# A 3x3 convolution with 2x2 max pooling: a new program order, 21 column maxima as one reduction, and sums placed on other engines

## The chip, the core and the metric

The kernel runs on one core of one Trainium2 chip. The core has five engines, each with a queue of its own that it works through in order: TensorE (PE in the profile; its weight loads are shown as PEld), VectorE (DVE), ScalarE (ACT), GpSimd (POOL) and SyncE (SP). An instruction waits for semaphores that other engines raise, and all that stands behind it in its queue waits with it. The metric is device time in microseconds. The time of a kernel is the median of several executions, and one further execution is profiled. The span of the profile runs from the first to the last instruction of the core.

## What is computed

The input x is 16 images of 64 channels and 64x64 points, the weight is 128x64x3x3. The kernel convolves with a border of one zero and takes the maximum of each 2x2 block:

```python
x_pad = np.pad(x, ((0, 0), (0, 0), (1, 1), (1, 1)))
...
conv[b, co] += weight[co, ci, kh, kw] * x_pad[b, ci, kh:kh+h, kw:kw+w]
...
output[b, c, i, j] = np.max(conv[b, c, 2*i:2*i+2, 2*j:2*j+2])
```

The output is 16x128x32x32 in float32, and on the chip x and the weights are rounded to bfloat16.

## The kernel before

**Tiles.** Two images lie on the 128 partitions together, 64 channels each, so there are 8 pairs of images (`xb_0` to `xb_7`). Each pair is cut into 4 strips of 16 rows, which gives 32 strips. Strip s belongs to pair s // 4; strips 2 and 3 trade places. For a strip and a half h (one image of the pair), 8 pooled rows of 64 columns fill one PSUM bank of 512 float32 numbers. There are 8 banks, and the program hands them out from a list of free ones (`take`, `free`).

**Products.** A strip needs the even and the odd convolution rows, and only their maximum counts. Both share a common part, which is added after the maximum of rows, because max(u+c, v+c) = max(u, v)+c. In a strip of type K (strips 0, 2, 4, 10, 16, 23) there are five products for each half: PA1 and PA2 into one bank, PB1 and PB2 into another, and PR, the common part, on the sum of rows `ks`. In a strip of type W (the other 26) there are four: P2 on a difference of rows (`we`, step E), P0 and P3 on a larger difference (`wd`, step D), P1 on a sum of rows (`ws`, step S). A product is three matmuls (kernel columns 1, 0 and 2; 512, 504 and 504 output columns, line 182). The matmul of half 0 and that of half 1 use different rows of the array and are issued in turn, one of each; `product` (line 236) holds a product back until the other half has one too. The first three strips (F, H, G) and the last (Z, Q) use products over half a strip.

**Steps of a strip after TensorE.** SE (line 356, ACT) copies the bank of P2 to a second bank, so that P0 adds to the one and P3 to the other. EV (lines 340 and 342, ACT) copies the first bank to SBUF as `ev` and frees it. MX (line 376, DVE) takes the maximum of the second bank and `ev` in place, and P1 (or PR) then adds to it. OD (line 382, ACT) copies the odd columns, 256 numbers per partition, to `od`. CM (line 396, DVE) takes the maximum of the even columns in PSUM and `od` into the output tile `o`, and frees the bank. ST (line 416) stores a strip over SP's queue. The output tiles are a ring of 12 (line 61): the 13th strip's first CM waits until the first strip's store has landed.

**Engines of the sums.** E, S, D and the halves Ea, Eb, Da, Db of strip 1 run on DVE or, where `ON_GPSIMD` names them, on POOL. A sum on POOL is made to wait for the last sum that stands before it in the order on DVE (`behind`, lines 74 to 84).

**Weights and loads.** The weights arrive in one transfer, are cast (g0, g1, g2), combined (D2, D0, GS, GM, GP), transposed on TensorE (TD2 to TMP, line 149) and copied back from PSUM (VD2 to VMP, lines 164 to 168) by ACT or DVE. The loads of x are issued by POOL (line 105): seven for pair 0 (La to C), two or three for each other pair (LX.p.part). So a load also waits its turn in POOL's queue.

**Order.** All of this is one list of 749 steps, `ORDER`, written out by hand, and each engine's queue is the part of the list that concerns it. At the start 8 matmuls on constants (line 524) run before any data is there.

Of the kernel before, what the change touches and what calls it, by code (L numbers as in the profile page):

```python
# [11 lines left out]
def kernel(  # L12
# [451 lines left out]
    for m in PRODUCTS:  # L464
# [13 lines left out]
        OD.3.1 CM.3.1 E.7 P2.7.0 P2.7.1 SE.7.0 P1.5.1 P1.5.0 S.9 S.6 P1.6.0 LX.5.0 P1.6.1 S.7 SE.7.1 P3.7.0
        P0.7.0 E.11 E.9 P2.9.0 PA1.10.0 OD.5.0 CM.5.0 OD.6.1 CM.6.1 E.13 OD.5.1 CM.5.1 OD.6.0 CM.6.0 KS.10 D.13
        S.14 E.8 P0.7.1 EV.7.1 P3.7.1 MX.7.1 EV.7.0 MX.7.0 P2.9.1 SE.9.0 PA1.10.1 PA2.10.1 SE.9.1 P0.9.1 P3.9.1  # L480
        PA2.10.0 EV.10.0 D.11 S.8 S.11 P0.9.0 EV.9.0 P3.9.0 MX.9.0 PB1.10.0 P1.7.1 PB1.10.1 PB2.10.0 PB2.10.1
        P2.8.1 EV.9.1 MX.9.1 OD.7.1 CM.7.1 P1.7.0 P1.9.0 P1.9.1 P2.13.0 MX.10.0 PR.10.0 P2.8.0 EV.10.1 MX.10.1
        PR.10.1 PA1.16.0 PA2.16.0 OD.7.0 CM.7.0 ST.0 ST.2 ST.6 D.8 SE.8.1 OD.9.0 CM.9.0 P0.8.1 LX.5.1 S.13
        LX.6.0 OD.9.1 CM.9.1 OD.10.0 CM.10.0 OD.10.1 CM.10.1 ST.10 PA1.16.1 PA2.16.1 D.17 D.12 D.14 S.15 P3.8.1
        SE.8.0 P0.8.0 EV.8.1 MX.8.1 SE.13.0 EV.16.1 EV.16.0 EV.8.0 P3.8.0 P0.13.0 P2.11.1 PB1.16.1 P2.11.0
        PB2.16.1 E.17 EV.13.0 P1.8.1 SE.11.1 P0.11.1 P3.11.1 P3.13.0 MX.8.0 P1.8.0 SE.11.0 P0.11.0 P3.11.0 E.20
        KS.16 MX.16.1 PR.16.1 MX.13.0 OD.8.1 CM.8.1 OD.8.0 CM.8.0 EV.11.1 MX.11.1 EV.11.0 MX.11.0 P2.13.1
        OD.16.1 CM.16.1 P1.13.0 OD.13.0 CM.13.0 PB1.16.0 PB2.16.0 E.14 P2.14.1 P1.11.0 P2.14.0 P1.11.1 SE.13.1
        P0.13.1 MX.16.0 SE.14.1 P3.13.1 P0.14.1 OD.11.1 CM.11.1 OD.11.0 CM.11.0 E.15 E.18 LX.6.1 E.12 P3.14.1
        PR.16.0 P2.12.1 P2.12.0 EV.13.1 SE.14.0 P0.14.0 D.18 KS.23 MX.13.1 P1.13.1 P3.14.0 EV.14.1 MX.14.1  # L490
        P1.14.1 S.19 S.20 SE.12.0 P0.12.0 EV.14.0 MX.14.0 SE.12.1 P3.12.0 P0.12.1 OD.16.0 CM.16.0 EV.12.0
        MX.12.0 OD.14.1 CM.14.1 EV.12.1 OD.13.1 CM.13.1 ST.5 ST.13 P3.12.1 P1.14.0 OD.14.0 CM.14.0 ST.14 ST.7
        ST.16 ST.3 P2.18.0 S.12 P1.12.0 P2.15.0 P2.17.1 PA1.23.1 SE.18.0 PA2.23.1 MX.12.1 P1.12.1 OD.12.0
        CM.12.0 E.19 S.17 LX.7.0 LX.7.1 D.15 D.20 D.24 SE.17.1 EV.23.1 P0.18.0 P0.17.1 EV.18.0 SE.15.0 OD.12.1
        CM.12.1 P3.18.0 MX.18.0 P3.17.1 P2.17.0 PB1.23.1 P2.18.1 PB2.23.1 EV.17.1 MX.17.1 P1.17.1 P0.15.0
        SE.17.0 P3.15.0 EV.15.0 MX.15.0 SE.18.1 P0.18.1 P0.17.0 P3.17.0 S.18 P1.18.0 P1.15.0 P3.18.1 MX.23.1
        P2.15.1 EV.17.0 MX.17.0 P1.17.0 PR.23.1 OD.17.1 CM.17.1 OD.18.0 CM.18.0 EV.18.1 MX.18.1 PA1.23.0
        PA2.23.0 P1.18.1 OD.15.0 CM.15.0 OD.17.0 CM.17.0 ST.11 ST.12 ST.9 S.22 D.25 E.22 D.19 S.24 SE.15.1
        OD.23.1 OD.18.1 CM.18.1 P2.20.0 P0.15.1 P2.19.1 PB1.23.0 PB2.23.0 P3.15.1 E.25 EV.23.0 CM.23.1 SE.20.0
        P0.20.0 P3.20.0 MX.23.0 PR.23.0 P2.19.0 P2.20.1 SE.19.1 P0.19.1 P3.19.1 EV.15.1 MX.15.1 P1.15.1 EV.20.0  # L500
        MX.20.0 P1.20.0 SE.20.1 P0.20.1 P2.22.0 OD.23.0 CM.23.0 ST.23 ST.18 ST.8 EV.19.1 MX.19.1 OD.15.1 CM.15.1
        SE.19.0 P0.19.0 P3.20.1 EV.20.1 MX.20.1 SE.22.0 OD.20.0 P1.19.1 D.21 E.21 P3.19.0 P2.22.1 D.22 P0.22.0
        P3.22.0 P1.20.1 E.24 CM.20.0 S.26 EV.19.0 MX.19.0 P2.21.1 P1.19.0 OD.19.1 CM.19.1 SE.22.1 P0.22.1
        P3.22.1 OD.20.1 CM.20.1 ST.20 S.29 EV.22.0 MX.22.0 SE.21.1 P2.24.0 P0.21.1 P3.21.1 EV.22.1 MX.22.1
        P2.21.0 OD.19.0 CM.19.0 P1.22.0 P1.22.1 SE.24.0 P0.24.0 EV.21.1 MX.21.1 OD.22.0 CM.22.0 P2.24.1 P2.25.1
        P3.24.0 SE.21.0 OD.22.1 CM.22.1 S.25 S.21 S.28 P0.21.0 P3.21.0 P2.25.0 P1.21.1 E.26 E.28 EV.24.0 MX.24.0
# [59 lines left out]
```

## Time and profile before

| what | before |
|---|---|
| median of 3 executions | 101.95 us (101.53 to 102.34) |
| profiled execution | 101.44 us, of it the span 99.7 us |
| busy, of the span | PE 94.1, PEld 60.8, DVE 86.2, ACT 83.2, POOL 72.8 us |
| mean granted TensorE clock | 0.99 |
| DMA | 17.23 MB, mean 173 GB/s |

The profiled execution lies 0.51 us below the median. What lies outside the span (1.7 us) is taken as fixed. An engine that is busy all the time need not be the one that sets the end; for that one looks at who waits for whom. The busy time of a group is given with the mean duration of one instruction; where instructions of an engine follow one another directly, each starts some 0.05 to 0.1 us before the one ahead of it has ended, so what an instruction occupies is the distance of two starts.

### The profile page before, as it was taken

The numbers are of one execution on the slowest core, as the hardware profiler recorded it, in microseconds if no ns is written. First come the engines' busy times: TensorE is split into PE (matmuls) and PEld (weight loads), VectorE is DVE, ScalarE is ACT, GpSimd is POOL, SyncE is SP. The second block draws the span as 40 slices with busy tenths as digits, with TensorE's granted clock in tenths as the row PEclk, the third lists the DMA queues.
The fourth block names the chain that finished last, engine by engine and source line by source line (L and its number), as shares of the span: only waits on it lengthen the run. The fifth ranks groups of instructions, "written<-read, shape, count | busy, mean of one in ns | idle before, by whom it ended". The sixth has DMA issues, their size and how long they took to land.

```text
span 99.7 us, 2526 instructions
## 1 busy us (share of the span) xinstructions
PE 94.1 (94%) x913; PEld 60.8 (61%) x913; DVE 86.2 (86%) x192; ACT 83.2 (83%) x192; POOL 72.8 (73%) x74
## 2 busy tenths in 40 slices
PE   6999999999999999999999999999999999998830
...
DVE  3568899999999999999999999889896899888660
...
GB/s 57 167 170 157 184 203 208 205 221 207 227 230 230 263 276 197 183 229 77 144 3 285 147 205 227 357 187 180 105 105 7 68 268 193 0 217 105 138 202 81
DMA packets 12316, 17.23 MB, mean 173 GB/s; under 512 B 912, under 2 KB 10256, under 8 KB 12304
## 3 DMA queue, kind: packets, MB, share of 16 engines
...
q8 instruction: 7, 0.11, 0.5%
...
## 4 chain that ended last, share of the span: by engine, by line
PE 83%; ACT 9%; DVE 3%; issue 1%; DVEq 0%; ACTq 0%
PE acc L182 78%; ACT ev L342 4%; PE acc L524 4%; ACT acc L356 3%; PE acc L149 2%; ACT od L382 2%; DVE acc L376 1%; DVE acc L372 1%; DVE o L396 0%; DVE o L410 0%; ACT od L402 0%; DVEq L561 0%; DVEq L376 0%; ACTq L356 0%
## 5 line engine op out<-in xcount | busy, mean ns | idle before, releaser
L182 PEld LDWEIGHTS <-wt 64*128 64x128 bf16 x882 | 57.8, 94 | 31.5 <-issue 3.9
L182 PE MATMUL acc<-wd,wt 64*128 64x512 bf16 (+3 forms) x330 | 60.0, 365 | 0.0
L376 DVE TENSOR_TENSOR acc<-acc,ev 128x512 f32<-128x512 f32 x62 | 41.4, 694 | 3.8 <-ACT ev L342 2.0
L182 PE MATMUL acc<-ws,wt 64*128 64x512 bf16 (+3 forms) x162 | 37.4, 369 | 1.0 <-DVE acc L372 0.7
L182 PE MATMUL acc<-we,wt 64*128 64x512 bf16 (+3 forms) x162 | 36.6, 369 | 0.0
L342 ACT ACTIVATE ev<-acc 128x512 f32<-128x512 f32 x52 | 31.0, 617 | 0.6 <-PE acc L182 0.3
L356 ACT COPY acc<-acc 128x512 f32<-128x512 f32 x48 | 28.3, 595 | 3.1 <-DVE o L396 1.6
L396 DVE TENSOR_TENSOR o<-acc,od 128x256 f32<-128x256 f32 x62 | 24.5, 417 | 1.9 <-ACT od L382 1.3
L89 POOL TENSOR_TENSOR ws<-xb 128x512 bf16<-128x512 bf16 x18 | 20.6, 1155 | 6.5 <-PE acc L182 4.5
L89 POOL TENSOR_TENSOR we<-xb 128x512 bf16<-128x512 bf16 x17 | 19.5, 1154 | 7.6 <-DVE wd L88 3.9
L382 ACT COPY od<-acc 128x256 f32<-128x256 f32 x62 | 22.7, 389 | 2.2 <-PE acc L182 1.6
L89 POOL TENSOR_TENSOR wd<-xb 128x1024 bf16<-128x1024 bf16 (+1 forms) x10 | 20.3, 2030 | 5.2 <-DVE we L88 5.2
L182 PE MATMUL acc<-xb,wt 64*128 64x252 bf16 (+7 forms) x192 | 23.9, 319 | 0.0
L105 POOL DMA_DIRECT2D xb<-in_x_dram x22 | 12.2, 567 | 0.8 <-POOLq L547 0.8
L88 DVE TENSOR_TENSOR wd<-xb 128x1024 bf16<-128x1024 bf16 (+1 forms) x17 | 10.8, 667 | 0.0
L340 ACT COPY ev<-acc 128x512 f32<-128x512 f32 x12 | 6.7, 595 | 3.1 <-PE acc L182 3.1
L182 PE MATMUL acc<-ks,wt 64*128 64x504 bf16 (+1 forms) x36 | 7.3, 377 | 0.0
L524 PE MATMUL acc<-const-bfloat16-1.0 128*128 128x512 bf16 x8 | 3.6, 625 | 0.8 <-PEq L547 0.8
L88 DVE TENSOR_TENSOR we<-xb 128x512 bf16<-128x512 bf16 (+1 forms) x10 | 3.7, 391 | 0.0
L88 DVE TENSOR_TENSOR ws<-xb 128x512 bf16<-128x512 bf16 x8 | 3.3, 418 | 0.0
L88 DVE TENSOR_TENSOR ks<-xb 128x512 bf16<-128x512 bf16 x6 | 2.6, 438 | 0.7 <-DMA xb<-in_x_dram 0.7
L524 PEld LDWEIGHTS <-const-bfloat16-1.0 128*128 128x128 bf16 x8 | 1.0, 136 | 2.4 <-issue 2.4
...
## 6 DMA issues: line engine op xcount, KB each, us to landing
...
```

Source lines behind the costliest of these rows:

```text
L88: return on_vector(nc.vector.tensor_tensor(**args))
L89: return on_gpsimd(nc.gpsimd.tensor_tensor(**args))
L105: nc.gpsimd.dma_start(out=xb[p][:, 1 + lo : 1 + hi, :], in_=rows_of(p, lo, hi))
L149: nc.tensor.transpose(tp[:, k * CO : (k + 1) * CO], wq[:, j : j + 2, :].rearrange("a b c -> a (b c)"), ident,)
L182: nc.tensor.matmul(acc[t][:, i0:i1, o0:o1], wt[lo : lo + CI, m0 + kw - h, :], rows(lo, i0, i1, c0, c1), start=start and kw == 1, stop=True ...
L340: nc.scalar.copy(out=ev[s, h], in_=acc[t])
L342: nc.scalar.mul(ev[s, h], acc[t], -1.0)
L356: nc.scalar.copy(out=acc[tb[s, h]], in_=acc[ta[s, h]])
L376: nc.vector.tensor_tensor(out=t, in0=t, in1=ev[s, h], op=MAX)
L382: nc.scalar.copy(out=od[s, h], in_=acc[tb[s, h]][:, :, 1::2])
L396: nc.vector.tensor_tensor(out=ot[s][:, h], in0=acc[t][:, :, 0::2], in1=od[s, h], op=MAX)
L524: nc.tensor.matmul(acc[n].rearrange("p a b -> p (a b)"), ones[:, 0:128], ones, start=True, stop=True, skip_group_check=True)
```

## The change

- `REDUCED` was empty and now names 21 (strip, half) pairs. For these OD is left out, and CM is one `tensor_reduce` with maximum over pairs of neighbouring columns: it reads all 512 numbers of the bank and writes 256 (lines 388 to 395, present before but not reached).
- `ON_GPSIMD`: E.9, E.20, E.25, E.26, E.28, S.1, S.7, S.19, S.20 and Db go from DVE to POOL; E.5, S.5, S.18, S.25, S.27, S.28 and Da go from POOL to DVE. GS goes from POOL to DVE.
- ACT takes over the cast g1 and the copies VG1, VG2 and VMP from DVE.
- The list has the same 749 steps in another order.
- `last_start` and the branches for a last strip of type K are new, but the last strip stays W and no step Y stands in the list, so they change no instruction.

Some facts of the two lists. TensorE gets the same 882 matmuls; the last 126, from P2.27 on, stand in the same order except that P1.28.1 and P2.29.1 trade places. Between MX.13.0 and MX.26.0, both included, in the middle of the list:

| steps from MX.13.0 to MX.26.0 | before | after |
|---|---|---|
| matmuls from the end of P3.13.0 to the end of P3.26.0 | 354 | 354 |
| DVE: MX / CM as maximum / CM as reduction | 30 / 30 / 0 | 30 / 14 / 16 |
| DVE: sums D / other sums | 5 / 9 | 5 / 7 |
| ACT: EV / SE / OD | 28 / 25 / 30 | 27 / 25 / 13 |

The stores of the first strips stand later in the list: before, ST.4 and ST.1 stand just after CM.4.0, and after, the first ones (ST.3 ST.2 ST.0 ST.1) stand after CM.10.0.

The diff, with the list cut to its first and last lines and to those that the prediction speaks of:

```diff
@@ -38,13 +38,13 @@
 
     TYPES = "KWKWKWWWWWKWWWWWKWWWWWWKWWWWWWWW"
     ON_GPSIMD = """
-        Da E.3 S.3 E.5 S.5 E.6 E.7 S.9 S.6 E.13 D.11 S.8 S.11 S.13 E.17 E.14 E.15 E.18 E.12 S.12 E.19 S.17 S.18
-        S.22 D.25 E.22 D.21 E.21 D.22 S.26 S.25 S.21 S.28 D.26 D.28 E.27 E.29 D.27 E.30 S.27 D.30 S.30 E.31 D.31
-        S.31
+        Db S.1 E.3 S.3 E.7 E.6 S.6 E.9 S.7 E.13 S.9 S.8 S.11 D.11 S.13 S.20 E.14 E.12 E.17 S.17 E.18 E.20 E.15
+        S.12 S.19 E.19 S.22 E.22 E.29 D.25 D.22 E.21 D.21 E.28 E.27 S.21 E.25 E.26 D.26 S.26 D.28 D.27 E.30 D.30
+        E.31 S.30 D.31 S.31
     """.split()
-    TURNED_BY_SCALAR = ("D2", "G0", "D0")
-    CAST_BY_SCALAR = ("g0", "g2")
-    REDUCED = ()
+    TURNED_BY_SCALAR = ("D2", "G1", "G0", "D0", "G2", "MP")
+    CAST_BY_SCALAR = ("g0", "g1", "g2")
+    REDUCED = ((5, 0), (8, 0), (11, 1), (16, 0), (14, 1), (12, 0), (23, 1), (18, 1), (23, 0), (20, 0), (19, 1), (20, 1), (19, 0), (21, 1), (24, 0), (21, 0), (24, 1), (25, 0), (26, 1), (30, 0), (30, 1))
@@ -261,11 +261,20 @@
 
     def last_product(part):
         span = (0, R // 2) if part == 0 else (R // 2, R)
-        pair_of_taps(tb, (N - 1, part), GP, step1(row["s", N - 1]), False, None, span)
+        block = GP if TYPES[N - 1] == "W" else G1
+        pair_of_taps(tb, (N - 1, part), block, step1(row["s", N - 1]), False, None, span)
+
+    def last_start(part):
+        span = (0, R // 2) if part == 0 else (R // 2, R)
+        take(tb, (N - 1, part), 0)
+        take(tb, (N - 1, part), 1)
+        pair_of_taps(tb, (N - 1, part), D0, k_rows(N - 1, 0), True, None, span)
 
     def last_edges(part):
         span = (0, R // 2) if part == 0 else (R // 2, R)
-        pair_of_taps(tb, (N - 1, part), G2, step2(row["d", N - 1], 1), False, None, span)
+        w = TYPES[N - 1] == "W"
+        rows = step2(row["d", N - 1], 1) if w else k_rows(N - 1, 2)
+        pair_of_taps(tb, (N - 1, part), G2, rows, False, None if w else R - 1, span)
 
...
-        "GS": lambda: sbuf_sum(False, out=gsum, in0=g0, in1=g2, op=ADD),
+        "GS": lambda: sbuf_sum("GS" not in ON_GPSIMD, out=gsum, in0=g0, in1=g2, op=ADD),
...
-        "SL": seed_last, "Z": last_edges, "ML": rowmax_half, "U": last_store,
+        "SL": seed_last, "Y": last_start, "Z": last_edges, "ML": rowmax_half, "U": last_store,
...
-        La Lb A1 D2 g0 ID TD2 D0 TG0 g2 g1 TG2 A2 B1 B2 GS C LX.1.0 LX.1.1 LX.1.2 LX.2.0 LX.2.1 TG1 TD0 VD2
-        F.0.0 F.0.1 VG0 F.1.0 F.1.1 VG2 GP GM TMP VD0 H.0.0 H.1.1 VG1 H.1.0 H.0.1 EV.2.1 EV.2.0 EV.0.1 H.2.0
-        H.3.0 H.2.1 H.3.1 KS.2 VMP Ea KS.0 S.1 G.0.0 Eb G.0.1 F.2.0 F.3.1 MX.2.0 PR.2.0 F.3.0 F.2.1 MX.2.1
-        PR.2.1 Da Db D.3 EV.0.0 MX.0.0 SEa.0 SEa.1 SEb.1 SEb.0 G.2.1 G.1.1 G.1.0 MX.0.1 PR.0.1 OD.2.0 OD.2.1
-        CM.2.1 CM.2.0 EV.1.0 PA1.4.1 PB1.4.1 G.2.0 MX.1.0 PA2.4.1 EV.1.1 MX.1.1 PR.0.0 LX.3.0 E.3 S.3 LX.3.1 E.5
-        LX.4.0 LX.4.1 PB2.4.1 PA1.4.0 P2.3.0 PA2.4.0 P1.1.1 P1.1.0 P2.5.1 OD.0.1 CM.0.1 OD.0.0 CM.0.0 KS.4 D.5
-        SE.3.0 EV.4.1 MX.4.1 OD.1.0 CM.1.0 PB1.4.0 EV.4.0 PB2.4.0 MX.4.0 OD.1.1 CM.1.1 S.5 D.6 SE.5.1 P0.3.0
-        P2.3.1 P3.3.0 PR.4.1 EV.3.0 MX.3.0 SE.3.1 OD.4.1 CM.4.1 P0.5.1 PR.4.0 OD.4.0 CM.4.0 ST.4 ST.1 E.6 EV.5.1
-        D.7 D.9 P0.3.1 P3.3.1 P2.5.0 SE.5.0 EV.3.1 P1.3.0 OD.3.0 CM.3.0 MX.3.1 P2.6.1 P3.5.1 P2.6.0 P0.5.0
...
-        OD.29.0 CM.29.0 ST.29 S.30 E.31 P2.31.1 P2.31.0 SL.1.0 SL.1.1 SL.0.0 SL.0.1 P1.30.0 P1.30.1 OD.30.0
-        CM.30.0 OD.30.1 CM.30.1 ST.30 ST.26 D.31 P0.31.0 P0.31.1 Z.0 EV.31.0 ML.0.0 EV.31.1 ML.0.1 Z.1 ML.1.1
-        ML.1.0 S.31 Q.0 ODh.0.1 CMh.0.1 ODh.0.0 CMh.0.0 U.0 Q.1 ODh.1.0 ODh.1.1 CMh.1.0 U.1 CMh.1.1 U.2
+        La Lb ID A1 A2 B1 D2 g0 TD2 D0 TG0 GS GM GP KS.0 KS.2 Ea Da B2 C LX.1.0 LX.1.1 LX.1.2 LX.2.0 LX.2.1 Eb
+        Db g1 TG1 g2 TG2 TD0 VD2 F.0.0 TMP VG1 VG0 F.1.1 F.0.1 H.0.0 H.1.0 VD0 VG2 VMP H.2.0 F.2.0 F.1.0 EV.0.0
+        EV.0.1 H.1.1 H.0.1 H.3.0 H.3.1 H.2.1 EV.2.0 MX.2.0 G.0.0 G.0.1 F.2.1 PR.2.0 EV.2.1 MX.2.1 D.3 F.3.1
+        F.3.0 MX.0.0 MX.0.1 SEa.0 SEa.1 SEb.1 SEb.0 PR.2.1 OD.2.1 CM.2.1 OD.2.0 CM.2.0 G.1.0 G.1.1 G.2.1 EV.1.0
+        G.2.0 MX.1.0 PR.0.0 PR.0.1 EV.1.1 MX.1.1 OD.0.0 CM.0.0 OD.0.1 CM.0.1 PB1.4.0 PA1.4.1 PA2.4.1 PB1.4.1
+        PA1.4.0 PB2.4.1 S.1 P1.1.1 P1.1.0 EV.4.1 OD.1.0 E.3 P2.3.0 SE.3.0 S.3 KS.4 D.5 S.5 E.5 P2.5.1 CM.1.0
+        MX.4.1 PA2.4.0 EV.4.0 PB2.4.0 MX.4.0 OD.1.1 CM.1.1 LX.3.0 LX.3.1 LX.4.0 E.7 D.6 P0.3.0 P2.3.1 PR.4.1
+        SE.5.1 P3.3.0 P0.5.1 EV.3.0 MX.3.0 SE.3.1 P0.3.1 OD.4.1 CM.4.1 PR.4.0 OD.4.0 CM.4.0 E.6 EV.5.1 D.9 D.7
...
+        SE.8.1 D.8 P0.8.1 OD.9.0 CM.9.0 OD.9.1 CM.9.1 PR.10.0 OD.10.0 CM.10.0 ST.3 ST.2 ST.0 ST.1 OD.10.1
...
+        P3.28.0 OD.26.1 CM.26.1 ST.26 SE.27.0 EV.28.0 MX.28.0 SE.27.1 D.27 P0.27.0 EV.27.0 E.30 S.27 D.29
...
+        D.30 P0.30.0 P0.30.1 P3.30.1 EV.30.0 P3.30.0 MX.30.0 P1.29.0 OD.29.1 CM.29.1 EV.30.1 MX.30.1 OD.29.0
+        CM.29.0 E.31 P2.31.1 S.30 P1.30.1 P2.31.0 SL.0.0 P1.30.0 OD.30.0 CM.30.0 SL.0.1 OD.30.1 CM.30.1 ST.30
+        ST.29 SL.1.0 D.31 SL.1.1 P0.31.1 P0.31.0 EV.31.0 Z.0 ML.0.0 EV.31.1 ML.0.1 Z.1 ML.1.0 ML.1.1 S.31 Q.0
+        ODh.0.0 CMh.0.0 ODh.0.1 CMh.0.1 U.0 Q.1 ODh.1.0 ODh.1.1 CMh.1.0 U.1 CMh.1.1 U.2
     """
```

More of the change, by code (lines that the diff above doesn't have):

```diff
@@ L478 @@
[L478 to L506, printed above, removed]
-        P1.24.0 SE.24.1 P0.24.1 P3.24.1 EV.21.0 MX.21.0 OD.21.1 SE.25.1 P0.25.1 CM.21.1 P3.25.1 EV.24.1 MX.24.1
@@ new lines @@
+        EV.16.1 P0.13.0 P2.11.0 P3.13.0 PB2.16.1 SE.11.1 EV.13.0 SE.11.0 P0.11.1 EV.11.1 P3.11.1 MX.8.0 P1.8.0
+        OD.8.0 P0.11.0 MX.8.1 P1.8.1 OD.8.1 MX.16.1 PR.16.1 P2.13.1 MX.13.0 MX.11.1 CM.8.0 CM.8.1 P3.11.0
+        EV.11.0 MX.11.0 P1.13.0 OD.13.0 CM.13.0 PB1.16.0 P1.11.1 PB2.16.0 OD.16.1 CM.16.1 OD.11.1 CM.11.1 S.20
+        E.14 P2.14.1 E.12 E.17 S.17 E.18 MX.16.0 SE.13.1 P0.13.1 P3.13.1 P1.11.0 SE.14.1 P0.14.1 P2.14.0 P3.14.1
+        P2.12.0 OD.11.0 CM.11.0 D.18 KS.23 PR.16.0 P2.12.1 EV.13.1 MX.13.1 SE.14.0 P0.14.0 OD.16.0 EV.14.1
```

43 lines of the change are left out of this document (33 added, 10 removed).

## The prediction

> **What bounds the kernel now.** First the page: busy times, the slices, the chain that ended last. Then the chain in order of time, and the table by windows.
>
> ```profile
> PE 94.1 (94%) x913; PEld 60.8 (61%) x913; DVE 86.2 (86%) x192; ACT 83.2 (83%) x192; POOL 72.8 (73%) x74
> PE   6999999999999999999999999999999999998830
> DVE  3568899999999999999999999889896899888660
> PE 83%; ACT 9%; DVE 3%; issue 1%; DVEq 0%; ACTq 0%
> ```
>
> ```profile
> 7.74 74.25 PE acc L182 x735
> ```
>
> ```profile
> 20.00:80.00 60.00, 60.00 (x556) 38.67 (x554) 57.14 (x120) 55.98 (x129) 44.69 (x38) 1.00 0.78 182
> ```
>
> The chain runs for 74.25 us through TensorE alone. Between 20 and 80 us TensorE is never idle and its granted clock is 1.00; 556 matmuls in 60.00 us are 0.108 us each, two abreast. A busy PE is no proof of PE at its peak, so I look for what it waited for between 8 and 90 us:
>
> ```profile
> PEld L182 <- DVE o L396: 0.5, 2, 0.3
> PEld L182 <- DVE wd L88: 0.3, 1, 0.3
> PEld L182 <- ACT acc L356: 0.2, 1, 0.2
> ```
>
> Waits of the weight loads, which run ahead of the matmuls, add up to 1.0 us, and that is the most that a better order can win in the body. The number of matmuls does not change, so this part is fixed at the pace of 0.108 us.
>
> The last part:
>
> ```profile
> 89.90 2.14 POOL L89 TENSOR_TENSOR wd<-xb 128x1024 bf16<-128x1024 bf16 x1
> 90.34 1.00 PE L182 MATMUL acc<-we,wt 64*128 64x512 bf16 x6
> 91.24 1.19 ACT L367 COPY acc<-acc 128x256 f32<-128x256 f32 x4 [0.23 <-PE acc L182]
> 91.70 0.81 PE L182 MATMUL acc<-ws,wt 64*128 64x512 bf16 x5 [0.33 <-DVE acc L376]
> 92.21 1.73 PE L182 MATMUL acc<-wd,wt 64*128 64x512 bf16 x18
> 93.12 1.08 ACT L342 ACTIVATE ev<-acc 128x512 f32<-128x512 f32 x2
> 93.75 1.58 DVE L372 TENSOR_TENSOR acc<-acc,ev 128x256 f32<-128x256 f32 x4 [0.24 <-ACT ev L342]
> 95.39 0.51 PE L182 MATMUL acc<-ws,wt 64*128 64x256 bf16 x6 [0.18 <-DVE acc L372]
> ```
>
> P2.31 ends, four half copies (SL) follow on ACT, P0.31 may write only after them, then two EV, four half maxima, Q.0 and Q.1, the column maxima and the store. Each waits for the one before.
>
> **The change part by part.** Durations first, groups kept apart by form, then rows from which the distance of two starts is read:
>
> ```profile
> L376 DVE TENSOR_TENSOR acc<-acc,ev 128x512 f32<-128x512 f32 x62 | 41.4, 694 | 3.8 <-ACT ev L342 2.0 <-ACT ev L340 0.5 <-ACT acc L356 0.3
> L396 DVE TENSOR_TENSOR o<-acc,od 128x256 f32<-128x256 f32 x62 | 24.5, 417 | 1.9 <-ACT od L382 1.3
> L382 ACT COPY od<-acc 128x256 f32<-128x256 f32 x62 | 22.7, 389 | 2.2 <-PE acc L182 1.6
> L88 DVE TENSOR_TENSOR wd<-xb 128x1024 bf16<-128x1024 bf16 x16 | 10.5, 683 | 0.0
> L88 DVE TENSOR_TENSOR ws<-xb 128x512 bf16<-128x512 bf16 x8 | 3.3, 418 | 0.0
> L166 DVE TENSOR_SCALAR wt<-acc 128x896 bf16<-128x896 bf16 x1 | 0.6, 617 | 0.0
> L89 POOL TENSOR_TENSOR gsum<-wraw 128x192 f32<-128x192 f32 x1 | 0.8, 840 | 0.0
> L164 ACT COPY wt<-acc 128x384 bf16<-128x384 bf16 x2 | 1.0, 482 | 0.1
> ```
>
> ```profile
> 10.48 1.30 DVE L376 TENSOR_TENSOR acc<-acc,ev 128x512 f32<-128x512 f32 x2 [0.47 <-ACT ev L340]
> 13.82 0.75 DVE L396 TENSOR_TENSOR o<-acc,od 128x256 f32<-128x256 f32 x2
> 13.04 0.65 ACT L382 COPY od<-acc 128x256 f32<-128x256 f32 x2 [0.58 <-PE acc L182]
> 78.14 2.27 POOL L89 TENSOR_TENSOR we<-xb 128x512 bf16<-128x512 bf16 x2
> ```
>
> Two in 1.30 us, the second lasting 0.69: a row maximum occupies DVE for 0.61 us. In the same way a column maximum takes 0.33, an OD on ACT 0.26, a small sum on POOL 1.11; for DVE's sums I take 0.33 (418 less the same overlap of 0.08) and 0.60 (683 less 0.08).
>
> *The reductions.* No trace line shows one. It reads 512 numbers of PSUM and writes 256. Bounds from the nearest rows: 0.33 us, if the numbers written count (the column maximum), and 0.61, if the numbers read count (the row maximum). I take 0.61, since the same bank is read in full there. Ends for the range: 0.33 below; above, if it works like the copy and the maximum one after the other, 0.33 + 0.39 = 0.72. With 0.61 DVE gains 21 x 0.28 = 5.9 us of work, and ACT loses 21 x 0.26 = 5.5 us.
>
> The Trainium skill (VectorE: DVE Perf Modes, The perf-mode tier table (the rule you actually need)) speaks against the change: it gives tensor_reduce the 1x mode alone, and the Rules for kernel authors there call it the slowest DVE operation on a hot path. By that rule the price is that of the numbers read, 5.9 us more on DVE; by the numbers written it would be 0. No trace line here shows which.
>
> *Is that on the path?* I count the middle of the list, MX.13.0 to MX.26.0, from the table in the section on the change. TensorE: 354 x 0.108 = 38.2 us. DVE before: 30 x 0.61 + 30 x 0.33 + 5 x 0.60 + 9 x 0.33 = 34.2 us. DVE after: 18.3 + 14 x 0.33 + 16 x 0.61 + 3.0 + 7 x 0.33 = 38.0 us. So DVE goes from 90% to 99% of TensorE's time, and nothing is left over, yet it does not pass it. The cover is thin: it is gone at 0.62 us a reduction, and from there each 0.1 us costs 16 x 0.1 = 1.6 us. Cost taken: 0, with TensorE's matmuls as what hides it.
>
> *Sums.* POOL gets three small sums more (39 for 36), 3.3 us, and loses GS, 0.84; DVE loses three, 1.0 us. POOL was busy for 72.8 of 99.7 us. A sum on POOL waits for the last sum before it on DVE, so late DVE makes POOL late. The tightest new place is the start: S.5 and E.5 now stand on DVE behind KS.4 and D.5, and P2.5.1 needs E.5.
>
> ```profile
> 16.53 0.53 DVE L88 TENSOR_TENSOR ks<-xb 128x512 bf16<-128x512 bf16 x1
> 17.97 0.38 PE L182 MATMUL acc<-we,wt 64*128 64x512 bf16 x1
> ```
>
> KS.4 starts at 16.53; with 0.33 + 0.60 + 0.33 + 0.33 E.5 is done at 18.12, and the product started at 17.97. Queued behind E.5 are CM.1.0 and MX.4.1. Cost 0 to 0.3, taken 0.1.
>
> *The head.* ACT takes g1, VG1, VG2 and VMP (0.62 on DVE, 896 columns). At ACT's 0.48 us for 384 columns that is 0.5 + 2 x 0.48 + 1.1 = 2.6 us; DVE is rid of them and gets GS. These rows hold what hides it:
>
> ```profile
> 1.24 1.75 POOL L105 DMA_DIRECT2D xb<-in_x_dram  x3 [0.79 <-POOLq L547]
> 4.14 1.70 PE L149 MATMUL acc<-ident,wq 128*128 128x128 bf16 x16
> 5.77 1.47 PE L182 MATMUL acc<-xb,wt 64*128 64x256 bf16 x24
> 7.67 0.50 PE L182 MATMUL acc<-xb,wt 64*128 64x256 bf16 x6
> 9.20 2.05 ACT L340 COPY ev<-acc 128x512 f32<-128x512 f32 x4 [2.85 <-PE acc L182]
> ```
>
> ```profile
> xb<-in_x_dram POOLq DMA_DIRECT2D x1, 160.0 KB, 4.4
> ```
>
> The 16 transposes ahead of F.0.0 stay, so the first product stays at 5.77. ACT was idle for 2.85 us ahead of its first EV, and that takes the 2.6. Within it the copies come in the order in which products need them: VG1 and VG0 after VD2, done at some 6.3, while F.1.1 comes after F.0.0 and the seven transposes of TMP, at about 6.6; VMP, the longest, ends at about 8, ahead of the first EV. If that cover were gone, a product would wait for its weights, 0.5 us for each copy in front of it. On POOL the identity now goes before A1, whose issue moves from 2.46 (third of three in 1.75 us) to some 3.05; with 4.4 us to landing (the load of 160 KB is A1) it is there at 7.45. H.0.0 needs it, and comes 6 half matmuls (0.3 us) earlier than its 7.67. Cost 0 to 0.3, taken 0.1. C and the loads of pairs 1 and 2 move earlier by GS and later by nothing. LX.3.0 now stands behind S.1, E.3 and S.3, LX.4.1 to LX.5.1 behind seven sums; what hides this is the row of loads already under way.
>
> *The tail.* The list is the same from P2.31 on but for SL's order, and POOL has one sum less (S.27) ahead of D.31. D.31 ended at 92.04, P0.31 started at 92.21, but also waited for SL, which starts at the end of P2.31. So that gain is 0; late next is SL. The two reductions of strip 30 (2 x 0.61 from about 92.4) end at 93.6, just ahead of the half maxima at 93.75.
>
> *Sum.* Head +0.1, E.5 +0.1, body between 0 and -1.0, taken -0.2 since ACT is lighter at the seeds, tail 0: 0.1 + 0.1 - 0.2 = 0, so 101.44 stays, or 101.4. The median of the runs shown lies 0.5 higher, for a reason that one execution does not show; for a median I add a little of it: **101.5 us**.
>
> **The rivals.** *DVE becomes the bound (slower).* For it: 99% in the middle, and the slices already show DVE at nine tenths or more from 20 to 65 us. Against it: idle DVE time between 60 and 90 us, which the change fills. It decides from 0.62 us a reduction. At the upper end of 0.72 it is 16 x 0.10 = 1.6 in the middle and 2 x 0.11 = 0.2 in the tail, 101.5 + 1.8 = 103.3. The warning in the Trainium skill (VectorE: DVE Perf Modes, Rules for kernel authors) would come true in this way; no run here shows it so far.
>
> *Output tiles come free late (slower).* The thirteenth strip's CM waits for the store of strip 2. The first stores were issued at 21.79; between 20 and 40 us, among loads, they took long:
>
> ```profile
> 21.79 7.74 SPq L416 DMA_DIRECT2D out_dram<-o  x5
> ```
>
> ```profile
> DMA to landing us min/median/max: 8.1/9.8/14.2
> ```
>
> Now they stand behind ST.3, and so behind CM.3.1. Matmul 840 starts at 90.34, so matmul N comes at about 90.34 - (840 - N) x 0.108: P1.3.1 ends with matmul 240, at 25.5, and CM.3.1 comes a microsecond or so later in DVE's full queue, so that the store is issued at about 27; PR.16.1 ends with matmul 402, at 43.0. 27 + 14.2 = 41.2, ahead of CM.16.1 at 43 to 44, so it decides if the store takes over 16 us. Each microsecond more then stops DVE, and soon TensorE, for as long. With 2 us: 103.5. For it: the loads of pairs 4 to 7 stand closer together in POOL's queue; against it: 2 us or more in hand.
>
> *The order wins (faster).* For it: the 1.0 us of waits at the weight loads, partly for column maxima that now need no copy, and ACT gets lighter: with 0.48 us for EV (two in 1.08 us at 93.12) and the same for SE, it falls in the middle from 53 x 0.48 + 30 x 0.26 = 33.2 to 52 x 0.48 + 13 x 0.26 = 28.3 us of 38.2. Against it: TensorE has no idle time there. All of it: 101.44 - 1.0 = 100.4.
>
> **How the numbers follow.** A measurement of this kernel can tell about 1% from no change, that is 100.93 and 102.97 around 101.95. Forecast (TensorE still sets the pace, 100.9 to 102.4): 0.55. DVE bound: 0.15, nearly all of it slower by over 1%. Stores: 0.08, slower. The order wins: 0.22, faster by over 1%. So faster 0.22, same 0.55, slower 0.23. The range 100.4 to 103.2 takes in the full gain and DVE's lateness up to 0.72 us a reduction.
>
> **What would show it.** Right: a chain still on PE, 20 to 80 us with 60.00 us of PE and about 556 matmuls, reductions starting 0.6 us apart, DVE at 59 of 60 us, ACT some 5 us lighter. Wrong: reductions at 0.7 us or more, waits of TensorE for MX or CM in the middle, a CM waiting for a store, or F.0.0 at another time than 5.8.

## The result, and the profile after

| | before | after |
|---|---|---|
| median | 101.93 us (101.53 to 102.47, 20 executions) | 102.28 us (101.77 to 102.79, 20 executions) |
| ratio to before, 95% interval | | 1.0043 [1.0027, 1.0059] |
| profiled execution, of it the span | 101.44 us, 99.7 us | 102.16 us, 100.4 us |

The change costs 0.35 us of the median. The forecast was 101.5 us and no change that can be told. The time lies inside the range, but what was forecast didn't come: the kernel became a little slower, where 101.5 lies a little below the kernel before. Between the two profiles there are 0.72 us, twice as much as between the medians, because the profiled execution before lay 0.49 us below its median and the one after only 0.12 below. So the profiles alone must not be differenced; which part of the 0.72 belongs to the change is the question of the experiments.

Lines of the file have moved by 9 behind the change: EV is now 349 and 351, SE 365, MX 385, OD 391, the reduction 398, CM as maximum 405. From the page of the kernel after, busy times, slices and the chain that ended last:

```profile
PE 94.8 (94%) x913; PEld 56.1 (56%) x913; DVE 88.2 (88%) x186; ACT 80.6 (80%) x175; POOL 75.2 (75%) x76
...
PE   6999999999999999999999999999999999998840
...
DVE  3551799999989999999999999999999999889860
...
PE 76%; DMA 7%; ACT 6%; POOL 3%; DVE 3%; issue 2%; DVEq 0%; POOLq 0%
```

A new name stands in the chain: DMA, 7% of the span, where before none stood. And DVE, full from the sixth slice on, is emptier than before in the third to fifth (about 5 to 12.5 us). The chain in order of time (start, duration, what):

```profile
3.07 1.54 POOL xb L105 x3
4.61 6.54 DMA xb<-in_x_dram
...
11.51 74.73 PE acc L182 x704
```

Before, TensorE carried the chain from 7.74. Now everything up to 11.15 hangs on a single load of x, issued at 4.61. It is B2, the sixth load of pair 0, and Eb waits for it, then G.0.1. TensorE and DVE around that place in the kernel after (start, duration, engine, line, tiles, count, idle before and what ended it):

```profile
6.10 0.50 PE L182 MATMUL acc<-xb,wt 64*128 64x256 bf16 x6
...
7.14 0.92 ACT L162 ACTIVATE wt<-acc 128x896 bf16<-128x896 bf16 x1
...
9.46 2.05 ACT L349 COPY ev<-acc 128x512 f32<-128x512 f32 x4 [1.40 <-PE acc L182]
10.34 0.29 DVE L88 TENSOR_TENSOR we<-xb 128x256 bf16<-128x256 bf16 x1 [1.80 <-DMA xb<-in_x_dram]
...
10.82 0.49 PE L182 MATMUL acc<-we,wt 64*128 64x256 bf16 x6
...
11.17 0.29 DVE L88 TENSOR_TENSOR we<-xb 128x256 bf16<-128x256 bf16 x1 [0.20 <-DMA xb<-in_x_dram]
...
11.51 0.51 PE L182 MATMUL acc<-we,wt 64*128 64x256 bf16 x6 [0.20 <-DVE we L88]
```

The two rows `we<-xb` on DVE are Ea and Eb; each starts in the moment its load is there, Ea after 1.80 us of idle DVE. Before, they started at 8.72 and 9.73, and the twelve matmuls of G ran without a break from 10.23. The loads of 128 KB are A2, B1 and B2, three in a group, and the row gives the median from issue to landing, which is B1's; before, it was 4.5. The second row is A1:

```profile
xb<-in_x_dram POOLq DMA_DIRECT2D x3, 128.0 KB, 6.2
...
xb<-in_x_dram POOLq DMA_DIRECT2D x1, 160.0 KB, 4.4
```

Now the middle, by windows (PE, PEld, DVE, ACT, POOL with busy time and count, clock, DMA share, GB/s), the kernel before:

```profile
7.00:9.00 2.00, 2.00 (x39) 1.58 (x34) 1.34 (x5) 0.00 (x0) 2.00 (x4) 1.00 1.05 157
...
41.00:79.00 38.00, 38.00 (x354) 25.88 (x353) 35.60 (x76) 36.22 (x83) 29.82 (x24) 1.00 0.63 155
```

and the kernel after:

```profile
7.00:9.00 2.00, 2.00 (x38) 1.77 (x38) 0.42 (x1) 1.06 (x2) 1.34 (x3) 1.00 0.99 90
20.00:80.00 60.00, 60.00 (x553) 34.42 (x550) 59.13 (x116) 52.09 (x111) 48.58 (x43) 1.00 0.72 174
41.00:79.00 38.00, 38.00 (x355) 21.69 (x352) 37.82 (x72) 32.68 (x68) 31.23 (x25) 1.00 0.58 157
```

In the middle TensorE is busy all the time, as before, with 355 matmuls for 354; DVE holds 37.82 of 38.00 us and still does not stop it. At 7 to 9 us the DMA engines are busy all the time in both kernels (share 0.99 and 1.05), but move 90 GB/s for 157. The groups of the column maximum in the kernel after, and two reductions in a row:

```profile
L405 DVE TENSOR_TENSOR o<-acc,od 128x256 f32<-128x256 f32 x41 | 16.2, 417 | 0.9 <-ACT od L391 0.7
L398 DVE TENSOR_REDUCE o<-acc 128x256 f32<-128x512 f32 x21 | 14.1, 682 | 0.4 <-PE acc L182 0.4
```

```profile
61.08 1.28 DVE L398 TENSOR_REDUCE o<-acc 128x256 f32<-128x512 f32 x2
```

1.28 less 0.68 is 0.60 us from one start to the next.

Where the 0.72 us come in, from the starts of TensorE's matmuls (N is the number in the order of issue):

| matmul | before | after | difference |
|---|---|---|---|
| 0, first product | 5.77 | 6.10 | 0.33 |
| 84, behind G | 10.89 | 11.51 | 0.62 |
| 120 | 13.18 | 13.80 | 0.62 |
| 480 | 51.24 | 52.08 | 0.84 |
| 840, P2.31 | 90.34 | 91.11 | 0.77 |
| end of the span | 99.7 | 100.4 | 0.7 |

All but 0.1 us is there by matmul 84. From 120 to 840 it takes 77.16 us before and 77.31 after. This small difference hides a second place: the 30 matmuls from 240 to 270, at about 26 to 29 us, take 3.24 us before and 3.53 after, and the rest of the stretch is 0.14 us shorter after than before. DVE there in the kernel after, then the weight loads, then DVE in e7, one of the experiments:

```profile
23.90 1.94 DVE L385 TENSOR_TENSOR acc<-acc,ev 128x512 f32<-128x512 f32 x3
26.04 1.30 DVE L385 TENSOR_TENSOR acc<-acc,ev 128x512 f32<-128x512 f32 x2 [0.20 <-issue]
```

```profile
27.39 0.55 PEld L182 LDWEIGHTS <-wt 64*128 64x128 bf16 x8 [0.40 <-DVE acc L385]
```

```profile
23.87 3.13 DVE L385 TENSOR_TENSOR acc<-acc,ev 128x512 f32<-128x512 f32 x5
```

Five row maxima follow one another. In the kernel after, DVE stands still for 0.20 us ahead of the fourth, for nothing that the profile shows (`issue`), and a weight load then waits 0.40 us for a row maximum. In e7, as in the kernel before, the five run without a break. TensorE's busy time doesn't show this place (60.00 us between 20 and 80 in both kernels); the count of matmuls does, 553 for 556.

### The profile page after: what moved, and what is told of

It is laid out like the page before. It is cut to its first block, busy times and chain, and to the rows that moved or that the text cites. A ratio compares the mean times of both kernels' runs of the same rounds, so it can differ in the third digit from the quotient of the medians.

```text
span 100.4 us, 2493 instructions
## 1 busy us (share of the span) xinstructions
PE 94.8 (94%) x913; PEld 56.1 (56%) x913; DVE 88.2 (88%) x186; ACT 80.6 (80%) x175; POOL 75.2 (75%) x76
## 4 chain that ended last, share of the span: by engine, by line
PE 76%; DMA 7%; ACT 6%; POOL 3%; DVE 3%; issue 2%; DVEq 0%; POOLq 0%
PE acc L182 76%; DMA xb<-in_x_dram 7%; ACT ev L351 3%; POOL xb L105 3%; ACT acc L365 2%; DVE acc L385 1%; ACT od L391 1%; DVE acc L381 1%; DVE we L88 0%; DVE o L405 0%; POOL ident masks.py:199 0%; DVE o L419 0%; ACT od L411 0%; POOL ident masks.py:197 0%; DVEq L570 0%
## 5 line engine op out<-in xcount | busy, mean ns | idle before, releaser
L182 PEld LDWEIGHTS <-wt 64*128 64x128 bf16 x882 | 53.1, 94 | 36.8 <-issue 3.4
L182 PE MATMUL acc<-wd,wt 64*128 64x512 bf16 (+3 forms) x330 | 62.1, 365 | 0.0
L365 ACT COPY acc<-acc 128x512 f32<-128x512 f32 x48 | 27.6, 583 | 4.6 <-PE acc L182 2.9
L89 POOL TENSOR_TENSOR we<-xb 128x512 bf16<-128x512 bf16 x21 | 24.0, 1153 | 4.6 <-DVE ws L88 1.8
L182 PE MATMUL acc<-xb,wt 64*128 64x252 bf16 (+5 forms) x192 | 25.5, 319 | 0.0
L89 POOL TENSOR_TENSOR ws<-xb 128x512 bf16<-128x512 bf16 x17 | 19.5, 1151 | 6.9 <-DVE wd L88 4.9
L391 ACT COPY od<-acc 128x256 f32<-128x256 f32 x41 | 14.6, 378 | 3.1 <-PE acc L182 2.8
L405 DVE TENSOR_TENSOR o<-acc,od 128x256 f32<-128x256 f32 x41 | 16.2, 417 | 0.9 <-ACT od L391 0.7
L398 DVE TENSOR_REDUCE o<-acc 128x256 f32<-128x512 f32 x21 | 14.1, 682 | 0.4 <-PE acc L182 0.4
L88 DVE TENSOR_TENSOR we<-xb 128x512 bf16<-128x512 bf16 (+1 forms) x6 | 2.2, 376 | 2.0 <-DMA xb<-in_x_dram 2.0
```

Of the source, the lines that this page charges most:

```text
L88: return on_vector(nc.vector.tensor_tensor(**args))
L89: return on_gpsimd(nc.gpsimd.tensor_tensor(**args))
L182: nc.tensor.matmul(acc[t][:, i0:i1, o0:o1], wt[lo : lo + CI, m0 + kw - h, :], rows(lo, i0, i1, c0, c1), start=start and kw == 1, stop=True ...
L365: nc.scalar.copy(out=acc[tb[s, h]], in_=acc[ta[s, h]])
L391: nc.scalar.copy(out=od[s, h], in_=acc[tb[s, h]][:, :, 1::2])
L398: nc.vector.tensor_reduce(out=ot[s][:, h], in_=acc[t].rearrange("p r (w two) -> p r w two", two=2), axis=mybir.AxisListType.X, op=MAX,)
```

## The experiments

Two theories to begin with. *Head*: the loads of pair 0 land later and G waits for them; the middle costs nothing. *DVE*: the 21 reductions fill DVE, and the loss is made by them.

**e1, the reductions taken out of the changed kernel.**

```diff
-    REDUCED = ((5, 0), (8, 0), (11, 1), ...
+    REDUCED = ()
```

> The changed kernel with an empty REDUCED: every strip has its copy OD on ACT and its column maximum on DVE again, order and engines as changed. Theory head (the loss of 0.35 us arises before matmul 84: products start later and G.0.1 waits for Eb, which waits for a load): the time stays at 102.2 to 102.5, a ratio of 1.003 to 1.006 to the kernel before, and the first product starts at about 6.1 again. Theory DVE (the reductions, 0.28 us more each on a full DVE, cost the time): 101.9 or less, a ratio of 1.000 or below, with TensorE gaining between matmul 84 and 840.

Measured: 111.46 us, ratio 1.0918 [1.0865, 1.0970], far outside of both. Its waits (in total, times, longest):

```profile
ACT od L391 <- PE acc L182: 9.9, 23, 1.1
...
DVE acc L385 <- ACT ev L351: 6.8, 14, 1.2
...
PE acc L182 <- ACT acc L365: 2.6, 7, 0.8
```

The list was made with 21 OD steps that do nothing, so they stand anywhere. As real copies they stop ACT until their product is done, EV and SE queue behind them, and DVE and TensorE wait for those. That is no undoing of the reductions: it tells that order and reductions belong together, and nothing on the two theories.

**e2, the kernel before with the 21 reductions only.** The old list, `REDUCED` as after.

> The kernel before, in its own order and on its own engines, with the 21 reductions alone. Theory head: 101.9, a ratio of 0.999 to 1.001, since TensorE's matmuls still hide a DVE that is fuller by 5.7 us. Theory DVE: 102.3 or more, a ratio of 1.003 or above, and more waits of TensorE for MX and CM.

Measured: 103.92 us, 1.0172 [1.0124, 1.0219]. Windows and waits:

```profile
41.00:79.00 38.00, 37.34 (x336) 22.76 (x333) 37.02 (x72) 31.66 (x66) 27.65 (x23) 1.00 0.62 155
```

```profile
ACT acc L365 <- DVE o L398: 2.4, 5, 0.8
```

Here TensorE is idle for 0.66 of 38 us, 336 matmuls are done for 354, and SE on ACT waits 2.4 us for banks that a reduction frees late (0.4 in the kernel after). From matmul 240 to 660 it takes 47.66 us; in the kernel before 45.46, in the kernel after 45.68. So the reductions do cost some 2 us in the old order, and the new order takes them in. That is what the new body does: it pays for the reductions that it was made for, and wins nothing beyond.

**e3 and e9, the changed kernel with the head of before.** The first 68 steps up to MX.0.0 as before, with GS and Da on POOL, Db and S.1 on DVE, casts and copies as before; the rest, reductions and all, as after. e9 is the same kernel once more.

```diff
-        La Lb ID A1 A2 B1 D2 g0 TD2 D0 TG0 GS GM GP KS.0 KS.2 Ea Da B2 C LX.1.0 LX.1.1 LX.1.2 LX.2.0 LX.2.1 Eb
+        La Lb A1 D2 g0 ID TD2 D0 TG0 g2 g1 TG2 A2 B1 B2 GS C LX.1.0 LX.1.1 LX.1.2 LX.2.0 LX.2.1 TG1 TD0 VD2
...
```

> The changed kernel with the head of the kernel before: the first 68 steps of the old list (to MX.0.0), GS and Da on POOL, Db and S.1 on DVE, casts and copies of the weights as before; all later steps in the new order with the reductions. Theory head: 101.9 or a little less, a ratio of 0.997 to 1.001, products start at about 5.8 and no wait for Eb. Theory DVE: 102.3, a ratio of 1.003 to 1.006.

> The kernel of e3 once more (the changed kernel with the head of the kernel before), on the same chip as the changed kernel itself: theory head gives 101.8, a ratio of 0.996 to 0.999 to the kernel before and 0.4 to 0.5 us below the changed kernel. If the new body (all from MX.0.0 on) gains as well as the head loses, the ratio to the kernel before stays below 1; if the body is neutral, it is 1.000.

Measured: e3 101.81 us, 0.9973 [0.9942, 1.0005]; e9 101.89 us, 1.0004 [0.9983, 1.0024], both over 12 executions. No loss against the kernel before is left, while the middle stays as full as in the kernel after, here in e3:

```profile
7.00:9.00 2.00, 2.00 (x37) 1.57 (x34) 1.15 (x3) 0.00 (x0) 2.00 (x5) 1.00 1.09 161
...
41.00:79.00 38.00, 38.00 (x354) 21.79 (x352) 37.82 (x72) 32.59 (x68) 31.22 (x26) 1.00 0.56 153
```

That speaks against *DVE* in the middle. For *head* it says less, since a second thing has changed with the head: DVE's pause at 26 us isn't there in e3 or e9, and from matmul 120 to 840 they take 77.10 and 77.11 us for 77.31 in the kernel after. The advantage over before that e3 seemed to have was not there in e9. In e9's profile B2 landed at 10.52, G.0.1 waited a little for Eb even with the old head, and matmul 84 started at 11.54, no earlier than in the kernel after (11.51):

```profile
11.22 0.51 PE L182 MATMUL acc<-we,wt 64*128 64x256 bf16 x6 [0.26 <-DVE we L88]
```

**e4, the kernel before with the head of after.** The first 66 steps as after, Db and S.1 on POOL, no reductions.

> The kernel before with the head of the changed kernel: the first 66 steps of the new list (to MX.0.0), Db and S.1 on POOL, Da and GS on DVE, all casts and copies of the weights on ACT; all later steps in the old order without reductions. Theory head: 102.3, a ratio of 1.003 to 1.006, products start at about 6.1 and G.0.1 waits for Eb. Theory DVE: 101.9, a ratio of 0.999 to 1.001.

Measured: 103.27 us, 1.0140 [1.0077, 1.0203], over three times the loss of the whole change. From the first product to matmul 84 it takes what the kernel after takes, 5.41 us, for 5.12 before. Behind that it isn't a clean transplant: S.1 now stands on POOL ahead of E.3, S.3, E.5 and S.5, which the old list has there too, and from matmul 120 to 240 it takes 13.43 us, for 12.12 before and 12.13 after. These 1.31 us are nearly the whole loss of 1.33, so e4 says nothing about *head*.

Next, which edit of the head. *Identity*: A1 is issued later, since ID stands ahead of it, and all behind it shifts. *Row of loads*: with GS off POOL, C and the loads of pairs 1 and 2 follow B2 without a break and share the DMA engines with it.

**e5, e6, e7: one edit of the head taken back in the changed kernel.** e5: ID behind A1. e6: GS on POOL between B2 and C. e7: both.

```diff
-        La Lb ID A1 A2 B1 D2 g0 ...
+        La Lb A1 ID A2 B1 D2 g0 ...
```

```diff
     ON_GPSIMD = """
-        Db S.1 E.3 ...
+        GS Db S.1 E.3 ...
...
-        La Lb ID A1 A2 B1 D2 g0 TD2 D0 TG0 GS GM GP KS.0 KS.2 Ea Da B2 C ...
+        La Lb ID A1 A2 B1 B2 D2 g0 TD2 D0 TG0 GS GM GP KS.0 KS.2 Ea Da C ...
```

> The changed kernel with the identity (ID) back behind A1 on POOL, as before the change; GS stays on DVE. Theory row of loads (without GS on POOL, the seven loads from B2 on are issued in one unbroken row and slow down the ones ahead of them): B1 still lands at about 10.1 us and B2 at 10.8, and the time stays at 102.2 to 102.4, a ratio of 1.003 to 1.005. Theory identity (A1 issued 0.55 us later shifts the loads behind it): B1 lands at 8.6 to 9.0, and the time is 101.8 to 101.9, a ratio of 0.997 to 0.999.

> The changed kernel with GS back on POOL, between the issues of B2 and C as before; the identity stays ahead of A1. Theory row of loads: B1 lands at 8.6 to 9.0 and B2 at 9.4 to 9.7, no wait of TensorE for Eb, and the time is 101.8 to 101.9, a ratio of 0.997 to 0.999. Theory identity: B1 still at about 10.1, the time 102.2 to 102.4, a ratio of 1.003 to 1.005.

> The changed kernel with both back, so that POOL's queue at the start is that of the kernel before; casts and copies of the weights stay on ACT and the order of products stays. If POOL's queue is the whole cause of the late head: 101.8 to 101.9, a ratio of 0.997 to 0.999, B2 lands at 9.4 to 9.7. If the weights on ACT cost something of their own: 102.0 or more.

Measured, 12 executions each: e5 101.84 us, 0.9998 [0.9976, 1.0020]; e6 101.80, 0.9994 [0.9976, 1.0012]; e7 101.80, 0.9997 [0.9982, 1.0013]. None of them shows a loss against the kernel before, so by the times one edit taken back is enough, and neither theory alone accounts for the loss. The kernel after did not run beside them, though: their intervals lie below that of the first comparison (1.0027 to 1.0059), but not below that of its repeat, e11. In e5's profile the loads come earlier, B2 at 10.10, and the matmuls of G run without a break:

```profile
9.30 0.29 DVE L88 TENSOR_TENSOR we<-xb 128x256 bf16<-128x256 bf16 x1 [0.81 <-DMA xb<-in_x_dram]
...
10.13 0.29 DVE L88 TENSOR_TENSOR we<-xb 128x256 bf16<-128x256 bf16 x1 [0.20 <-DMA xb<-in_x_dram]
```

```profile
10.68 0.82 PE L182 MATMUL acc<-we,wt 64*128 64x256 bf16 x12
```

One profile doesn't show that it is always so: in e10 below, with the same head, B2 landed at 10.82. In e6 B2 still lands late, at 10.58, but another wait stands ahead of G and hides that. GM on DVE now waits for GS on POOL, and the transposes TMP wait for GM and GP; e6's waits and the piece of its chain:

```profile
DVE wq L88 <- POOL gsum L89: 1.4, 1, 1.4
...
PEld L149 <- DVE wq L88: 1.4, 3, 0.8
```

```profile
5.16 0.84 POOL gsum L89
...
7.39 78.51 PE acc L182 x782
```

Matmul 84 starts at 11.44 here, and at 11.46 in e7, hardly earlier than in the profile of the kernel after. What these two profiles gain lies behind it: they don't have DVE's pause.

The wait for GS can also be seen in the times themselves. The executions of e7 lie between 101.78 and 101.86 us and eleven of e6's twelve between 101.78 and 101.94, where those of before and after are spread over a whole microsecond. GS stands behind six load issues on POOL, and the sixth, that of B2, starts between 4.58 and 4.62 us in every profile; B2 lands anywhere between 9.36 and 11.53.

**e8, the two edits in the kernel before.** ID ahead of A1, GS on DVE, nothing else.

```diff
-        La Lb A1 D2 g0 ID TD2 ...
+        La Lb ID A1 D2 g0 TD2 ...
...
-        "GS": lambda: sbuf_sum(False, ...
+        "GS": lambda: sbuf_sum("GS" not in ON_GPSIMD, ...
```

> The kernel before with the new start of POOL's queue alone: the identity ahead of A1 and GS on DVE, everything else as it was. If POOL's queue is the cause: B1 lands at about 10.1 and B2 at 10.8 us, and the time is 102.2 to 102.5, a ratio of 1.003 to 1.006. If not: 101.9, a ratio of 0.999 to 1.001.

Measured: 103.02 us, 1.0100 [1.0071, 1.0128]. The two edits alone make the old kernel slower, and by more than they do in the new order. TensorE, then the group of A2, B1 and B2:

```profile
9.20 2.39 PE L182 MATMUL acc<-xb,wt 64*128 64x256 bf16 x42 [0.84 <-DMA xb<-in_x_dram]
...
12.23 0.51 PE L182 MATMUL acc<-we,wt 64*128 64x256 bf16 x6 [0.32 <-DVE we L88]
```

```profile
xb<-in_x_dram POOLq DMA_DIRECT2D x3, 128.0 KB, 6.2
```

Here H.1.1 waits for A2 (it landed at 9.15), then G.0.1 for Eb, and matmul 84 starts at 12.56, for 10.89 before. The new list has other steps ahead of H.1.1 and does not pay the first of the two.

**e10, a thinner cover.** e5 with 14 more reductions, so that all 30 column maxima between MX.13.0 and MX.26.0 are reductions.

```diff
-    REDUCED = ((5, 0), ..., (30, 0), (30, 1))
+    REDUCED = ((5, 0), ..., (30, 0), (30, 1), (8, 1), (13, 0), (16, 1), (11, 0), (13, 1), (14, 0), (12, 1),
+               (18, 0), (15, 0), (17, 1), (17, 0), (15, 1), (22, 0), (22, 1))
```

> The kernel of e5 (the changed kernel, identity behind A1) with 14 more reductions: every column maximum between MX.13.0 and MX.26.0 is one, so 30 of 30 there. Theory thin cover (DVE's work is at 99% of TensorE's time in that part and 0.27 us more for each reduction comes through): 14 x 0.27 = 3.8 us more work against 0.3 us left, 104.5 to 105.5. Theory slack (TensorE's queue of finished sums and free banks hides a DVE that falls behind): under 102.8.

Measured: 105.07 us, 1.0311 [1.0273, 1.0350]: 3.2 us above e5, which ran in another set, for 14 x 0.27 = 3.8 us more of DVE work. Its middle and its waits:

```profile
41.00:79.00 38.00, 36.87 (x325) 19.45 (x322) 37.71 (x67) 26.23 (x49) 27.93 (x23) 1.00 0.57 155
```

```profile
ACT acc L365 <- DVE o L398: 4.9, 9, 1.2
...
PEld L182 <- DVE o L398: 1.3, 3, 0.8
```

DVE is as full as in the kernel after (37.71 for 37.82), and now it is TensorE that is short: 325 matmuls for 355. So the kernel after stands close to the point where DVE takes over.

**e11, the changed kernel once more**, beside e9 and e10.

> The changed kernel itself once more. Theory row of loads and identity: B1 lands after 10.0 and B2 after 10.6 us again, G.0.1 waits for Eb, a ratio of 1.003 to 1.006. If the late loads of its first profile were chance: B2 at about 9.5 and no wait for Eb.

Measured: 102.00 us (101.41 to 103.03, 12 executions), 1.0011 [0.9980, 1.0043]. Its profile shows the same wait, a chain that hangs on B2 again:

```profile
4.59 6.48 DMA xb<-in_x_dram
...
11.44 74.74 PE acc L182 x704
```

but the first product started at 5.63 here, not at 6.10. This set by itself would not tell the kernel from before; the 1.0043 rests on the 20 executions of the first comparison, and the two intervals overlap. Against e9, in the same set, it is 0.11 us slower.

The landings of all profiles in one table, by what POOL's queue holds ahead of them (us from the start of the span; A2, B1 and B2 are issued at about 3.5, 4.1 and 4.6 throughout):

| POOL's queue | A1 | A2 | B1 | B2 | C |
|---|---|---|---|---|---|
| before | 6.91 | 7.75 | 8.57 | 9.36 | 11.06 |
| as before: e2, e3, e9 | 6.85 to 7.09 | 7.46 to 7.95 | 8.75 to 9.86 | 9.40 to 10.52 | 11.27 to 12.26 |
| both back, e7 | 7.19 | 7.95 | 9.10 | 9.79 | 12.47 |
| ID back only, e5 and e10 | 7.35, 7.25 | 7.97, 8.55 | 9.28, 9.58 | 10.10, 10.82 | 11.20, 11.91 |
| GS back only, e6 | 7.77 | 8.56 | 9.92 | 10.58 | 11.86 |
| after, e11 | 7.41, 7.34 | 8.02, 9.04 | 10.31, 10.41 | 11.14, 11.07 | 12.24, 12.17 |
| as after: e1, e4, e8 | 6.76 to 8.13 | 8.90 to 9.18 | 10.04 to 10.27 | 10.69 to 11.53 | 11.79 to 12.63 |

The mean of B2 is 9.75 us over the five profiles with both edits as before (before, e2, e3, e9, e7) and 11.05 over the five with both as after: 1.3 us later, with A1 issued 0.55 us later and B2 not at all. C comes 0.8 us earlier in the queue and lands later on the mean (12.15 for 11.68). The two single edits lie between, and one profile varies by about as much as they differ.

How much of the time lies ahead of matmul 84, and how much behind? The median of its start is not measured. An estimate adds to the start in the profile what the median lies above the profiled execution, as if all behind matmul 84 took the same time in each execution (from 120 to 840 it does so to 0.01 us between after and e11, and between e3 and e9):

| | matmul 84, profile | matmul 84, median, estimate | 120 to 840 | 240 to 270 |
|---|---|---|---|---|
| before | 10.89 | 11.38 | 77.16 | 3.24 |
| after | 11.51 | 11.63 | 77.31 | 3.53 |
| e11, after again | 11.44 | 11.39 | 77.32 | 3.54 |
| e3, e9 | 11.04, 11.54 | 11.40, 11.47 | 77.10, 77.11 | 3.32, 3.33 |
| e5 | 11.01 | 11.14 | 77.39 | 3.58 |
| e6, e7 | 11.44, 11.46 | 11.45, 11.45 | 77.04, 77.04 | 3.24, 3.24 |
| e8 | 12.56 | 12.21 | 77.39 | 3.33 |

By this 0.25 of the 0.35 us lie ahead of matmul 84 and 0.10 behind it. Between e9 and e11 all of the 0.11 us lies behind it, and so does over half of what e6 and e7 have over the kernel after (0.27 of 0.48). So e3, e9, e6 and e7 do not isolate the head. e5 and e8 do show it: e5 has DVE's pause and still loses nothing, with matmul 84 earlier, and in e8 matmul 84 comes later by 0.83. The pause stands ahead of that row maximum in the profiles of after, e11, e5, e10 and e1 (0.20 to 0.25 us; in e5 and e1 the profile names TensorE and ACT as what ended it) and in no other: these five have the new order with GS on DVE.

## Why the prediction was wrong

**What failed: the head.** The step is "C and the loads of pairs 1 and 2 move earlier by GS and later by nothing", with a cost of the head taken at 0.1. It moved these loads and left A2, B1 and B2 where they were, since their issue does not move. But the loads share the DMA engines, which were busy all the time (share 1.05 before and 0.99 after, between 7 and 9 us): with seven loads issued in a row and A1 late, B2 lands 1.3 us later on the mean of five profiles. The step that needs it, Eb and with it G.0.1, wasn't looked at; only A1 was followed to its product, H.0.0, and for A1 the forecast was near (7.45 foreseen, 7.41 and 7.34 found). In place of 0.1 the two profiles show 0.62 up to matmul 84, the estimate for the medians is 0.25, and by themselves the two edits cost the kernel before 1.0% (e8). How much the head costs in this change is not settled: in e11 the estimate is nothing, and from first product to matmul 84 it takes 5.41 us in the kernel after and 5.81 in e11, but with the head of before also 5.11 to 5.54.

**What failed too: the body, taken -0.2.** From matmul 120 to 840 the kernel after needs 0.15 us more, not 0.2 less. The new order does win a little: 0.05 to 0.12 where DVE's pause is absent (e3, e9, e6, e7). With the pause 0.2 to 0.3 is lost between matmul 240 and 270 (3.53 us, for 3.24 to 3.33 without). The prediction counted DVE's cover in the middle alone; at 26 us DVE has five row maxima in a row, and nothing there hides a pause of 0.20 us from TensorE. The rival *the order wins*, with 1.0 us, thus failed; most of what the new order is worth the reductions use up (e2). Why DVE pauses there stays open.

**The start.** The first product was to stay at 5.77 and came at 6.10. The forecast named that as a sign of a wrong step, but it is none: with either head it lay between 5.50 (e2) and 6.10 over the profiles, 6.01 in e9 and 5.63 in e11.

**The time as a number.** The sum ended at 101.4 for "no change" from a profile 0.49 us below its own median, and 0.1 of that was added. The median of "no change" was 101.93. So of the 0.78 us between 101.5 and 102.28, 0.43 are this and 0.35 the change. (The upper end of the range, 103.2, also lies 0.1 below the 103.3 that the prediction's own sum gives for a late DVE.)

**The price of a reduction, right.** 0.61 taken, 0.60 measured, the price of the numbers read. The Trainium skill (VectorE: DVE Perf Modes, The perf-mode tier table (the rule you actually need)) gives tensor_reduce the 1x mode only, and the trace agrees: 682 ns against 694 for the row maximum, which reads as many numbers of a bank.

**DVE in the middle, right.** 38.0 of 38.2 us were foreseen, 37.82 of 38.00 measured; 59 of 60 us, and 59.13. ACT became 3.9 us lighter there (55.98 to 52.09) where some 5 were expected. Thin but enough was the right reading for the middle: no TensorE time is lost there in the kernel after, and e10 shows the loss that comes as soon as the cover is used up. The rival *DVE becomes the bound* didn't happen in the middle, but in e2 and e10 it did, though not by a dearer reduction as it supposed: in e2 by the order, in e10 by the number of them. The Trainium skill (VectorE: DVE Perf Modes, Rules for kernel authors) warns of tensor_reduce on a hot path as the slowest DVE operation. The warning holds in e10, where 14 more of them cost 3.2 us; that it is the slowest does not hold here (682 ns for 694 of the row maximum).

**E.5, taken 0.1.** No wait of a product for E.5 is to be seen in the profile after. Matmul 108 to 240, where P2.5.1 lies, takes 13.11 us for 13.10 before. So it was 0.

**The tail, 0, right**: 9.25 us from P2.31 to the end of the span, for 9.33. **The stores:** no row among the waits of the kernel after names a store, so that rival did not decide.

**What stays open.** Why B1 and B2 land over a microsecond later when A1 is issued 0.55 later and the later loads follow without a break. Fewer bytes per busy DMA time is what the windows show (90 GB/s after, 78 in e11, 114 in e5, 111 in e6, 152 in e7, 161 in e3 between 7 and 9 us); the packets there have about the same size (310 000 bytes in 303 packets before, 180 000 in 196 after), so each takes longer. Whether it is the order of the pieces or the place of the target was not tried. Open are also the share of each of the two edits, what the head costs in the median, and what DVE's pause comes from.
